# Weight sums made one block ahead, and on VectorE for one triple only; the first head pair's cache and queries split earlier; x at the head of the loads

## The chip, the cores and the metric

The kernel runs on one core of a Trainium2 chip. The metric is device time in microseconds (us) of one execution, of which lower is better. A core has a tensor engine (PE in the profile; PEld is its weight load), VectorE (DVE), ScalarE (ACT), GpSimd (POOL) and SyncE (SP), each with an instruction queue of its own that runs in order, and 16 DMA engines that are fed from the queues of SP and, in a few places, of ACT.

## The reference

One step of a streaming encoder with one layer (D = 1024), for a prompt of 1024 frames and a sample of 32 more, all of it float32. What the kernel must compute, cut to what matters here:

```python
mod = silu(c) @ w_ada + b_ada                 # c_prompt for the prompt, c_sample for the sample
sh1, sc1, gt1, sh2, sc2, gt2 = split(mod, 6)
h = rmsnorm(x, g_mix) * (1 + sc1) + sh1
u = h @ w_in        # attention q, k, v; mLSTM q, k, v, o and gates; two merge gates
ya = sample or prompt band attention(q, k, v, rel_bias)   # 8 heads of 64, 64-frame chunks, 8 past ones
ym = mLSTM(...)                                # 4 heads of 128
x = x + gt1 * ((sigmoid(ga) * (ya @ w_br_att) + sigmoid(gm) * (ym @ w_br_mlstm)) @ w_out)
h2 = rmsnorm(x, g_ffn) * (1 + sc2) + sh2
g, up = split(h2 @ w_gate_up, 2)               # D_FF = 2816, that is 22 blocks of 128
x = x + gt2 * ((silu(g) * up) @ w_down)
y = rmsnorm(x, g_final)
```

The new keys and values, the mLSTM states and the convolution rows are outputs as well.

## The kernel before

**Tokens and tiles.** Prompt and sample are worked on together as T = 1056 tokens, with channels on the partitions and tokens along the free axis, in three thirds of 352 tokens (`TILES`).

**Products.** Every large product is done in three passes. Each operand is split in two: the high part is a copy rounded to the `fp32r` type, the low part is the float32 value less that copy. The passes are high by high, low by high, high by low (`PASSES`). `split_to` (lines 392 to 395) makes the two parts of a weight block: ACT writes the high part at line 394, and at line 395 VectorE (or GpSimd) subtracts it from the raw block. The profile's rows for L394 and L395 are these two steps, for all weights.

**Order of the work.** PE, ACT, VectorE and GpSimd run their instructions in the order in which the program traces them. The order on SP is chosen by the framework. `Weights.advance` loads a weight block's DRAM rows ahead and traces its split so that at most four blocks are split and not used up; `W.use` calls it ahead of each product. So block n + 3 is split in trace order just ahead of the product of block n, and the copies of product n out of PSUM come behind that split. `Side` mixes jobs written as generators (attention, mLSTM, the rest of the modulation) into the products, a step at a time; short tasks in `side.later` are taken out one by one between the matmuls of a unit (lines 434 and 435: at k = 2, 4 and 6, so three to a unit).

**The start** (lines 215 to 353). SP issues `c_prompt` and `c_sample` (lines 216 and 217, rows of `prow`), then the first four of eight tiles of x (line 231), the other six parameter vectors (`param_loads`, lines 220 to 225, also rows of `prow`), x tiles 4 to 7, the sample's x (line 235), and w_ada (line 286). PE transposes x with the identity, for each group of four x tiles eight times four transposes (line 300); ACT copies each four out of PSUM (line 301); VectorE makes the sums of squares (line 295). Behind the first two fours of the second group, `param_cols` transposes `prow` (line 245), and ACT takes silu of c (line 247). Then `first_ada` multiplies w_ada, PE for the larger part of it (line 337) and VectorE for the rest (lines 341 and 343, summed by PE at line 351), with the splits of the first two input weights in the midst of it (L394, L395). `first_units` (line 460) is the first product with h.

**The first head pair** (`b_qkv(0)`, then `attention(0)`). `k_block`, `v_block` and `q_block` project keys, values and queries of two heads. `q_block(0)` calls `cache_loads` (line 572; the loads are at lines 609 to 611) and, behind its three units, puts `cache_kv` into `side.later` (line 586). `cache_kv` transposes the cached keys (line 620) and splits cached keys and values (lines 624 and 626, and `split_heads`, lines 545 and 546). The first step of `attention(0)` computes the low part of the scaled queries on VectorE, as two instructions over all 1056 tokens (lines 644 and 645, tile `q_low`). The scores (line 667) multiply the high and then the low queries with the keys; their row minimum is taken at line 681 on VectorE.

**The fifteen products** (class `Fifteen`, lines 1306 to 1368, and `fifteen_products`). For 18 of the 22 blocks of the feed-forward layer, three 128-column rows of w_gate_up are multiplied at a time with a form that needs fifteen block products instead of eighteen. There are twelve such triples. Each has fifteen weight blocks of 512 x 128; the first four are blocks as they are loaded, the other eleven are sums or differences of blocks, made in place in the raw tiles at line 1362 by the engine `self.eng`, directly ahead of the block's split:

```python
            def split(_):
                if 3 in loads:
                    self.load(3)
                if op is not None:
                    self.eng.tensor_tensor(a(dst), a(x), a(y), op=op)
                t = wsplit_tile()
                split_to(t, a(dst))
                return [t]
```

Line 1397 gives the first two triples VectorE and the other ten GpSimd. The split's low part (L395) is on VectorE in this part of the kernel. Each product is twelve matmuls (line 1725); its result is copied out by ACT (line 1761) or added or subtracted on VectorE (line 1763, once a copy at line 1759); finished thirds go through silu (line 1788) and are multiplied (line 1792). From the last plain unit to the ninth product of the first triple, `late_forms` splits the last twenty pieces of the other operand too (ACT at line 1574, VectorE at line 1577); all of them are traced ahead of the ninth product. Behind the triples come the last block, the down projection and the final norm, which the change leaves alone.

Of the kernel before, what the change touches and what calls it, by code (L numbers as in the profile page):

```python
# [12 lines left out]
ALU = mybir.AluOpType  # L13
# [4 lines left out]
P = 128  # L18
# [121 lines left out]
def hybrid_stream_step(  # L140
# [55 lines left out]
    def f(ap):  # L196
        return ap.bitcast(F32)
# [15 lines left out]


    prow = tmpt((P, P))
    sp.dma_start(prow[R_C:R_C + 8], c_prompt.rearrange("o (r c) -> (o r) c", c=P))
    sp.dma_start(prow[R_C + 8:R_C + 16], c_sample.rearrange("o (r c) -> (o r) c", c=P))
    xtok = []
    def param_loads():
        sp.dma_start(prow[R_ADA:R_ADA + 48], b_ada.rearrange("o (r c) -> (o r) c", c=P))  # L220
        sp.dma_start(prow[R_GMIX:R_GMIX + 8], g_mix.rearrange("o (r c) -> (o r) c", c=P))
        sp.dma_start(prow[R_GFFN:R_GFFN + 8], g_ffn.rearrange("o (r c) -> (o r) c", c=P))
        sp.dma_start(prow[R_GAIN:R_GAIN + 4], mh_gain.rearrange("o (r c) -> (o r) c", c=P))
        sp.dma_start(prow[R_CW:R_CW + 32], conv_w.rearrange("o j (r c) -> (o j r) c", c=P))
        sp.dma_start(prow[R_CB:R_CB + 8], conv_b.rearrange("o (r c) -> (o r) c", c=P))

    for i in range(KD):
        if i % 2 == 0:
# [298 lines left out]
    def v_block(hp):  # L527
        w = w_cols(VA + hp * P)

        def run():  # L530
            vf = tmpt()
            for lo, hi, pt in units(w):
                act.activation(vf[:, lo:hi], pt, AF.Copy)
            W.advance()
            side.later += [lambda: v_tail(hp, vf, 0), lambda: v_tail(hp, vf, 1), lambda: v_sample(hp, vf)]
        run.w = w
        return run

# [21 lines left out]
    def v_sample(hp, vf):  # L560
        vst = vst_t[hp] = ap_.tile([TS, 2, 2, DH], F32R, tag="vst", name=nm("vst"))
        stg = sample_tail(vf[:, S:T], new_v_s, hp)
        split_heads(vst, stg.rearrange("p (h d) -> p h d", h=2), dve)

    def q_block(hp):
        w = w_cols(QA + hp * P, None if hp else slots)

        def run():
            qt = att_q[hp] = slot([P, 2, T], F32R)
            raw = q_raw[hp] = tmpt()  # L570
            if hp == 0:
                ckv = cache_loads()
                ql = slot([P, 2, T], F32R)
                for hh, (u, v) in enumerate(ROWS):
                    pool.memset(f(ql[v, hh]), 0.0)
                q_low.append(ql)
            for lo, hi in TILES:
                pt = unit(w, 0, hs, lo, hi)
                act.activation(raw[:, lo:hi], pt, AF.Copy, scale=DH ** -0.5)

                for hh, (u, v) in enumerate(ROWS):
                    act.activation(qt[u, hh, lo:hi], pt[u], AF.Copy, scale=DH ** -0.5)
                for hh, (u, v) in enumerate(ROWS):
                    pool.tensor_scalar(qt[v, hh, lo:hi], f(qt[u, hh, lo:hi]), 1.0, 1.0, op0=ALU.mult, op1=ALU.mult)
            if hp == 0:
                side.later.append(lambda: cache_kv(ckv))
        run.w = w
        return run

# [48 lines left out]
    def attention(hp):  # L638
# [1 line left out]

        ck, cv = ckv_t
        kt, qt, vt, vst = att_k[hp], att_q[hp], att_v[hp], vst_t[hp]
        ql, raw = q_low[0], q_raw[hp]
        for hh, (u, v) in enumerate(ROWS):
            dve.tensor_tensor(ql[u, hh], raw[u], f(qt[u, hh]), op=ALU.subtract)
        yield
        yaT = tmpt()
        bts = {}
# [659 lines left out]
    class Fifteen:  # L1308
# [6 lines left out]
        def __init__(self, rows, eng):  # L1315
            self.rows, self.raw, self.eng = rows, {}, eng
            plus, minus = ALU.add, ALU.subtract
            p, q, r, s, t, u = [(i, j) for i in range(3) for j in range(2)]
            x = (3, 0)
            self.blocks = [  # L1320
                self.block(p, loads=(0, 1)),
                self.block(q),
                self.block(s, loads=(2,)),
                self.block(t),
                self.block(x, r, minus, s, loads=(3,)),
                self.block(r, p, minus, r),
                self.block(u, q, minus, u),
                self.block(r, r, plus, s),
                self.block(u, t, plus, u),
                self.block(s, s, minus, t),  # L1330
                self.block(t, q, minus, r),
                self.block(r, q, minus, u),
                self.block(p, p, minus, u),
                self.block(x, x, plus, s),
                self.block(s, s, minus, r),
            ]
# [12 lines left out]
        def block(self, dst, x=None, op=None, y=None, loads=()):  # L1349
# [5 lines left out]
                    if i < 3:  # L1355
                        self.load(i)

            def split(_):
                if 3 in loads:
                    self.load(3)  # L1360
                if op is not None:
                    self.eng.tensor_tensor(a(dst), a(x), a(y), op=op)  # L1362
                t = wsplit_tile()
                split_to(t, a(dst))
                return [t]
# [28 lines left out]
    w_f = [[weight([gate_up(c, fb)], KD, 3, slots if fb == 1 else None)  # L1394
            for c in range(2)] for fb in range(NPLAIN)]
    hk_rows = [gate_up(c, fb) for fb in range(NPLAIN, NF - 1) for c in range(2)]
    fifteen = [Fifteen(hk_rows[i:i + 3], dve if i < 6 else pool) for i in range(0, len(hk_rows), 3)]
    w_last = [last_blocks(gate_up(c, NF - 1)) for c in range(2)]

    def down(k0, k1, j):  # L1400
# [776 lines left out]
```

## Time and profile before

| | us |
|---|---|
| time, median of three runs (1637.7 to 1637.98) | 1637.95 |
| time of the profiled execution | 1636.14 |
| its span, first to last instruction | 1634.1 |
| PE busy | 1589.4 |
| VectorE busy | 1124.6 |
| ScalarE busy | 782.9 |
| GpSimd busy | 416.9 |

The mean granted clock of the tensor engine is 0.997. The profiled execution's time is 2.0 us above its span. A busy share of the tensor engine isn't a share of its peak: matmuls are pipelined, and one that stands alone shows 0.43 us where one in a row takes 0.16 us from start to start. Idle time of an engine counts only where PE waits for it in the end. In rows of the timeline the columns are start, duration, engine, line, operation, output <- input, shape, count, and in brackets the idle time ahead of it and what ended it. "L395" is line 395 of the kernel.

### The profile page before, as it was taken

What the parts mean: (1) busy time and instruction counts of PE and PEld (TensorE: products, weight loads), DVE (VectorE), ACT (ScalarE), POOL (GpSimd) and SP (SyncE); (2) the same over time, 40 slices, a digit from 0 to 9 for tenths busy, and PEclk for the clock granted to TensorE, in tenths of its full rate; (3) what the DMA queues carried; (4) which work ended last, traced back from release to release, by engine and by line L of the source; (5) the groups of instructions that cost most, each with busy time, mean ns of one, the idle gap of its engine ahead of it and who ended that gap; (6) DMA issues with size and microseconds to landing.
All of it is one profiled execution on the core that took longest, in us unless ns stands there. A gap on an engine that the chain in (4) does not pass through costs nothing.

```text
span 1634.1 us, 27464 instructions
## 1 busy us (share of the span) xinstructions
PE 1589.4 (97%) x10324; PEld 1564.6 (96%) x10324; DVE 1124.6 (69%) x2186; ACT 782.9 (48%) x1735; POOL 416.9 (26%) x451
## 2 busy tenths in 40 slices
PE   7989999999999999999999998899999999999997
PEld 6989999999999999999999997899999999999997
DVE  6756564546776744546655697789888886799754
ACT  3456454543455544443434555454454544545443
POOL 1234333334332311000012100056566560000001
PEclk9999999999999999999999999999999999999999
DMA  9732323232223332584453210222313227427454
GB/s 343 260 93 76 111 75 106 67 123 80 84 83 79 64 97 68 123 276 156 132 152 109 92 53 27 79 92 79 105 53 104 79 66 253 142 78 241 129 157 126
DMA packets 210326, 192.44 MB, mean 118 GB/s; under 512 B 10571, under 2 KB 180531, under 8 KB 209171
## 3 DMA queue, kind: packets, MB, share of 16 engines
q1 hardware_dynamic: 205554, 187.88, 36.9%
q10 hardware_dynamic: 4640, 2.82, 0.6%
q8 instruction: 81, 1.33, 0.3%
q14 instruction: 51, 0.41, 0.1%
HBM read 152.19 MB, written 41.63 MB: 119 GB/s over the span
## 4 chain that ended last, share of the span: by engine, by line
PE 85%; DVE 5%; ACT 3%; issue 1%; DMA 0%; ACTq 0%; POOL 0%; DVEq 0%; POOLq 0%
PE mm L428 39%; PE psb L1725 17%; PE mm L1725 9%; PE mm L2128 3%; PE mm L826 2%; PE psb L2128 2%; PE psV L725 2%; PE psb L1971 2%; PE psS L667 1%; PE psT L694 1%; PE mm L1971 1%; ACT wsp L394 1%; DVE wsp L395 1%; DVE st L681 1%; PE psV L1060 1%
## 5 line engine op out<-in xcount | busy, mean ns | idle before, releaser
L428 PE MATMUL mm<-s,wsp 128*128 128x352 f32 x4104 | 689.9, 324 | 2.1 <-DVE stg L518 1.6
L428 PEld LDWEIGHTS mm<-s,wsp 128*128 128x128 f32 x4104 | 656.9, 188 | 4.7 <-DVE stg L518 2.2
L395 DVE TENSOR_TENSOR wsp<-wraw,wsp 128x512 fp32r<-128x512 f32 (+1 forms) x284 | 234.1, 842 | 133.3 <-ACT wsp L394 131.6
L1725 PE MATMUL psb<-s,wsp 128*128 128x352 f32 x1611 | 273.5, 323 | 6.5 <-DVE t L1763 2.8
L394 ACT ACTIVATE wsp<-wraw 128x512 fp32r<-128x512 f32 x340 | 201.4, 617 | 156.0 <-PE psb L1725 40.4
L1725 PEld LDWEIGHTS psb<-s,wsp 128*128 128x128 f32 x1611 | 260.4, 188 | 9.5 <-ACT wsp L394 6.6
L1725 PE MATMUL mm<-s,wsp 128*128 128x352 f32 x933 | 161.3, 323 | 4.5 <-DVE wsp L395 1.7
L1725 PEld LDWEIGHTS mm<-s,wsp 128*128 128x128 f32 x933 | 151.1, 188 | 7.5 <-DVE wsp L395 3.2
L687 POOL TENSOR_SCALAR st<-st,mx 128x640 f32<-128x640 f32 (+5 forms) x72 | 56.2, 781 | 190.8 <-DVE mx L686 172.4
L1142 DVE SCALAR_TENSOR_TENSOR t<-wa,cmix,t 128x512 f32<-128x512 f32 x112 | 89.8, 807 | 11.9 <-DMA wa<-in_w_ada_dram 11.5
L395 POOL TENSOR_TENSOR wsp<-wraw,wsp 128x512 fp32r<-128x512 f32 x56 | 75.5, 1369 | 51.2 <-ACT wsp L394 50.7
L682 ACT ACTIVATE st<-st,mx 128x640 f32<-128x640 f32 (+5 forms) x72 | 47.9, 665 | 72.0 <-DVE mx L681 71.9
L681 DVE CUSTOM_DVE_ANT_0 st<-psS,bias 128x640 f32<-128x640 f32 (+5 forms) x72 | 44.5, 617 | 55.0 <-PE psS L667 42.6
L701 ACT ACTIVATE pT<-psT 128x640 fp32r<-128x640 f32 (+3 forms) x80 | 38.7, 494 | 69.2 <-PE psT L694 49.4
L1675 POOL TENSOR_TENSOR t<-t,sl 128x352 f32<-128x352 f32 x18 | 17.4, 968 | 185.3 <-ACT sl L1673 185.3
L2040 POOL TENSOR_TENSOR fst<-fst 128x1 f32<-128x1 f32 (+1 forms) x6 | 1.2, 192 | 236.9 <-ACT t L2033 236.9
L1362 POOL TENSOR_TENSOR spare<-wraw 128x512 f32<-128x512 f32 x10 | 14.5, 1447 | 172.4 <-DVE t L1763 138.7
L706 DVE TENSOR_TENSOR pT<-psT,pT 128x640 fp32r<-128x640 f32 (+3 forms) x80 | 44.0, 559 | 20.5 <-ACT pT L701 20.3
L826 PE MATMUL mm<-s,s 128*128 128x264 f32 (+3 forms) x432 | 54.8, 283 | 0.0
L2128 PE MATMUL mm<-s,wsp 128*128 128x352 f32 x330 | 54.4, 324 | 0.0
L2128 PEld LDWEIGHTS mm<-s,wsp 128*128 128x128 f32 x330 | 53.0, 188 | 0.0
L826 PEld LDWEIGHTS mm<-s,s 128*128 128x128 f32 (+1 forms) x432 | 51.9, 179 | 0.5
(384 smaller groups left out, 2539.2 us busy)
## 6 DMA issues: line engine op xcount, KB each, us to landing
wraw<-in_w_in_dram SPq DMA_DIRECT2D x40, 512.0 KB
wraw<-in_w_gate_up_dram SPq DMA_DIRECT2D x33, 512.0 KB
wa<-in_w_ada_dram SPq DMA_DIRECT2D x64, 256.0 KB
wraw<-in_w_down_dram SPq DMA_DIRECT2D x32, 512.0 KB
a_d<-t SPq DMA_DIRECT2D x22, 528.0 KB
g_d<-t SPq DMA_DIRECT2D x16, 528.0 KB
x<-xres SPq DMA_DIRECT2D x16, 528.0 KB
t<-g_d SPq DMA_DIRECT2D x16, 528.0 KB
```

The lines of the kernel that those rows point to most:

```text
L394: act.activation(dst[:, 0], src, AF.Copy)
L395: eng.tensor_tensor(dst[:, 1], src, f(dst[:, 0]), op=ALU.subtract)
L428: pe.matmul(pt[:, :hi - lo], wt[(w0 + k) // 4][:, a, (w0 + k) % 4], xt[k][:, b, lo:hi], start=(k == 0 and q == 0), stop=(k == n - 1 and q ...
L681: dve.tensor_tensor_reduce(so, sv, bi, -1.0, 3.0e38, ALU.add, ALU.min, mx[:n, 1:2])
L682: act.activation(st[:n, :w], st[:n, :w], AF.Exp, bias=mx[:n, 1:2], scale=-1.0, accum_out=mx[:n, 2:3])
L687: pool.tensor_scalar(st[:n, :w], st[:n, :w], mx[:n, 3:4], 1.0, op0=ALU.mult, op1=ALU.mult)
L706: dve.tensor_tensor(pv[:m, 1, a:b], pT[:m, a:b], f(pv[:m, 0, a:b]), op=ALU.subtract)
L826: pe.matmul(pt[:n, :wd], hs[k][:, a, i * P:i * P + n], whl[b][:, k, :wd], start=(k == 0 and q == 0), stop=(k == KD - 1 and q == 2))
L1142: dve.scalar_tensor_tensor(ac[:, c], wa, cmix[:, c, k:k + 1], ac[:, c], op0=ALU.mult, op1=ALU.add)
L1725: pe.matmul(acc, wt[:, a, k], x[k][:, b], start=(start and not onto and k == 0 and q == 0), stop=(stop and k == 3 and q == 2), skip_group_ ...
L1971: pe.matmul(acc, wt[k // 4][:, u, k % 4], piece_of[k, i][:, v], start=(k == 0 and q == 0), stop=(k == KP - 1 and q == 2))
L2128: pe.matmul(acc, wt[(k - k0) // 4][:, u, (k - k0) % 4], piece_of[k, 2][:, v], start=(k == 0 and q == 0), stop=(k == NF - 1 and q == 2))
```

## The change

1. **Sums.** Making a block's sum is taken out of `split` into `make`, and the makes are kept in a list. The split of block n first calls the make of block n + 1 of the same triple, then does its own two steps. So the sum of block n + 1 stands ahead of the low part of block n on VectorE, and one block earlier on GpSimd.
2. **Engine of the sums.** VectorE makes them in the first triple alone; the second triple's go to GpSimd, like those of the ten behind it.
3. **The first head pair.** `cache_loads` is called from `v_block(0)` and `cache_kv` is put into `side.later` behind that block's own three tasks, so that it is taken out in the third unit of `q_block(0)` instead of the first unit of `k_block(1)`. The low part of the queries of this pair is computed by thirds (`low_queries`, two instructions of 64 x 352 for each), each behind its unit in `q_block(0)`, and no longer in the first step of `attention(0)`. The other three pairs keep theirs.
4. **Loads.** The two c vectors go into `param_loads`, and all eight parameter loads are issued from ACT's queue. SP issues nothing ahead of the x tiles.

The hunks stand in the order of the code: the parameter loads, `v_block`, `low_queries`, `q_block`, the first step of `attention`, `Fifteen.block`, and the line that makes the triples. (In `Fifteen.__init__`, `self.sums = []` is added ahead of the blocks.)

```diff
@@ -213,16 +213,13 @@
     prow = tmpt((P, P))
-    sp.dma_start(prow[R_C:R_C + 8], c_prompt.rearrange("o (r c) -> (o r) c", c=P))
-    sp.dma_start(prow[R_C + 8:R_C + 16], c_sample.rearrange("o (r c) -> (o r) c", c=P))
     xtok = []
+
     def param_loads():
-        sp.dma_start(prow[R_ADA:R_ADA + 48], b_ada.rearrange("o (r c) -> (o r) c", c=P))
...
-        sp.dma_start(prow[R_CB:R_CB + 8], conv_b.rearrange("o (r c) -> (o r) c", c=P))
+        for row, src in ((R_C, c_prompt), (R_C + 8, c_sample), (R_ADA, b_ada), (R_GMIX, g_mix), (R_GFFN, g_ffn),
+                         (R_GAIN, mh_gain), (R_CB, conv_b)):
+            act.dma_start(prow[row:row + src.shape[-1] // P], src.rearrange("o (r c) -> (o r) c", c=P))
+        act.dma_start(prow[R_CW:R_CW + 32], conv_w.rearrange("o j (r c) -> (o j r) c", c=P))
...
@@ -529,10 +526,14 @@
         def run():
             vf = tmpt()
+            if hp == 0:
+                ckv = cache_loads()
             for lo, hi, pt in units(w):
                 act.activation(vf[:, lo:hi], pt, AF.Copy)
             W.advance()
             side.later += [lambda: v_tail(hp, vf, 0), lambda: v_tail(hp, vf, 1), lambda: v_sample(hp, vf)]
+            if hp == 0:
+                side.later.append(lambda: cache_kv(ckv))
...
@@ -562,6 +563,10 @@
+    def low_queries(hp, lo, hi):
+        for hh, (u, v) in enumerate(ROWS):
+            dve.tensor_tensor(q_low[0][u, hh, lo:hi], q_raw[hp][u, lo:hi], f(att_q[hp][u, hh, lo:hi]), op=ALU.subtract)
...
@@ -569,7 +574,6 @@
             if hp == 0:
-                ckv = cache_loads()
...
                 for hh, (u, v) in enumerate(ROWS):
                     pool.tensor_scalar(qt[v, hh, lo:hi], f(qt[u, hh, lo:hi]), 1.0, 1.0, op0=ALU.mult, op1=ALU.mult)
-            if hp == 0:
-                side.later.append(lambda: cache_kv(ckv))
+                if hp == 0:
+                    low_queries(hp, lo, hi)
...
@@ -640,9 +644,9 @@
-        ql, raw = q_low[0], q_raw[hp]
-        for hh, (u, v) in enumerate(ROWS):
-            dve.tensor_tensor(ql[u, hh], raw[u], f(qt[u, hh]), op=ALU.subtract)
+        ql = q_low[0]
+        if hp:
+            low_queries(hp, 0, T)
         yield
...
@@ -1355,11 +1360,19 @@
-            def split(_):
+            def make():
                 if 3 in loads:
                     self.load(3)
                 if op is not None:
                     self.eng.tensor_tensor(a(dst), a(x), a(y), op=op)
+
+            n = len(self.sums)
+            self.sums.append(make)
+
+            def split(_):
+
+                for f in self.sums[n + 1:n + 2]:
+                    f()
                 t = wsplit_tile()
                 split_to(t, a(dst))
                 return [t]
...
-    fifteen = [Fifteen(hk_rows[i:i + 3], dve if i < 6 else pool) for i in range(0, len(hk_rows), 3)]
+    fifteen = [Fifteen(hk_rows[i:i + 3], dve if i < 3 else pool) for i in range(0, len(hk_rows), 3)]
```

More of the change, by code (lines that the diff above doesn't have):

```diff
@@ L215, in hybrid_stream_step @@
     prow = tmpt((P, P))
-    sp.dma_start(prow[R_C:R_C + 8], c_prompt.rearrange("o (r c) -> (o r) c", c=P))
-    sp.dma_start(prow[R_C + 8:R_C + 16], c_sample.rearrange("o (r c) -> (o r) c", c=P))
     xtok = []
     def param_loads():
-        sp.dma_start(prow[R_ADA:R_ADA + 48], b_ada.rearrange("o (r c) -> (o r) c", c=P))
[L221 to L225, printed above, removed]
+        for row, src in ((R_C, c_prompt), (R_C + 8, c_sample), (R_ADA, b_ada), (R_GMIX, g_mix), (R_GFFN, g_ffn),
+                         (R_GAIN, mh_gain), (R_CB, conv_b)):
+            act.dma_start(prow[row:row + src.shape[-1] // P], src.rearrange("o (r c) -> (o r) c", c=P))
+        act.dma_start(prow[R_CW:R_CW + 32], conv_w.rearrange("o j (r c) -> (o j r) c", c=P))
     for i in range(KD):
@@ L1319, in __init__ @@
             x = (3, 0)
+            self.sums = []
             self.blocks = [
```

## Prediction, made before the change ran

> **What bounds the kernel now.** I read the page first (parts 1 and 2), then the waits of PE, then busy time by stretches, and then the timeline of the three places where PE has gaps. Page, part 1:
>
> ```profile
> PE 1589.4 (97%) x10324; PEld 1564.6 (96%) x10324; DVE 1124.6 (69%) x2186; ACT 782.9 (48%) x1735; POOL 416.9 (26%) x451
> ```
>
> PE is busy for 1589.4 of 1634.1 us, so an edit gains only where it takes a gap out of PE. Busy time by stretches (start:end, length, then busy us of PE, PEld, DVE, ACT, POOL, granted clock, DMA share, GB/s) shows where they are:
>
> ```profile
> 90.00:100.00 10.00, 7.80 (x48) 7.33 (x48) 7.80 (x16) 4.19 (x9) 2.23 (x6) 1.00 0.23 59
> 800.00:900.00 100.00, 100.00 (x631) 100.00 (x630) 55.79 (x100) 41.47 (x84) 16.22 (x16) 1.00 0.41 128
> 1000.00:1050.00 50.00, 41.27 (x231) 36.74 (x230) 37.03 (x69) 21.34 (x45) 0.00 (x0) 1.00 0.14 43
> 1050.00:1100.00 50.00, 46.91 (x284) 45.43 (x284) 42.91 (x65) 22.91 (x46) 22.20 (x14) 1.00 0.30 97
> 1600.00:1635.00 35.00, 24.51 (x162) 23.90 (x160) 14.25 (x26) 12.22 (x35) 4.60 (x14) 0.90 0.35 111
> ```
>
> PE is full from 800 to 900, for one, and has gaps at 90 to 100 (2.2 us), in 1000 to 1100 (8.7 and 3.1) and at the end (10.5 to 1635, which the change doesn't touch). The longest entry among PE's waits is the load of x (total, times, longest):
>
> ```profile
> PE mm L300 <- DMA s<-in_x_prompt_dram: 10.3, 6, 5.2
> ```
>
> The change goes at the start, at 90 to 100 and at 1000 to 1064. Busy time understates the last: the stretches of the first three triples there hold the same number of matmuls.
>
> ```profile
> 988.40:1029.60 41.20, 32.91 (x182) 28.81 (x181) 30.99 (x59) 18.98 (x41) 0.00 (x0) 1.00 0.21 64
> 1029.60:1064.00 34.40, 30.72 (x181) 28.78 (x180) 25.39 (x45) 13.57 (x27) 2.01 (x2) 1.00 0.21 63
> 1064.00:1093.10 29.10, 29.10 (x182) 28.82 (x181) 26.54 (x40) 14.41 (x29) 17.33 (x12) 1.00 0.28 92
> ```
>
> The third triple, with its sums on GpSimd, takes 29.10 us with PE full. The first takes 12.1 us more, the second 5.3. That 17.4 us is the largest thing the change can reach.
>
> **Part 1: sums a block ahead, first triple.** One round of the timeline:
>
> ```profile
> 1008.21 0.68 DVE L1362 TENSOR_TENSOR wraw<-wraw,wraw 128x512 f32<-128x512 f32 x1
> 1008.99 0.63 ACT L394 ACTIVATE wsp<-wraw 128x512 fp32r<-128x512 f32 x1 [1.47 <-DVE wraw L1362]
> 1009.65 0.69 DVE L395 TENSOR_TENSOR wsp<-wraw,wsp 128x512 fp32r<-128x512 f32 x1 [0.76 <-ACT wsp L394]
> ```
>
> VectorE makes a sum, ScalarE waits for it and copies the high part, and VectorE stands still for 0.76 us until it may subtract. The groups of VectorE within 988.4 to 1029.6 (count, busy, mean ns, then idle time ahead of them and its releaser) total it:
>
> ```profile
> L395 DVE TENSOR_TENSOR wsp<-wraw,wsp 128x512 fp32r<-128x512 f32 x13 | 8.9, 690 | 6.8 <-ACT wsp L394 6.8
> L1577 DVE TENSOR_TENSOR x<-x,x 128x352 fp32r<-128x352 f32 x9 | 4.5, 521 | 1.2 <-ACT x L1574 1.2
> L395 DVE TENSOR_TENSOR wsp<-spare,wsp 128x512 fp32r<-128x512 f32 x2 | 1.4, 692 | 1.5 <-ACT wsp L394 1.5
> ```
>
> Of VectorE's 10.2 idle us (41.20 less 30.99), 8.3 are this wait. After the change the next sum (0.68) stands between, while ScalarE copies (0.63) from a sum that is a round old, so the 8.3 go. Then VectorE needs 41.2 - 8.3 = 32.9 for this stretch, and PE 29.1. VectorE is last only while the late pieces (L1577) lie among its work. In the chain of work, which counts VectorE's instructions from start to start, a copy out of PSUM is 0.43 and a sum 0.61:
>
> ```profile
> 1004.08 0.86 DVE row L1763 x2
> 1005.81 0.61 DVE wraw L1362
> ```
>
> After the ninth product a block costs VectorE a sum, a low part of the same shape and about one copy, 0.61 + 0.61 + 0.43, near 1.7, against twelve matmuls in 29.1 / 15 = 1.94 on PE; over six blocks that returns up to 1.4. I take 32.0: **9.2 gained**. Most: 12.1, PE's floor. Least: 4, half of the waits, if ScalarE's copy then waits behind its own evictions instead. Nothing is below zero here: no instruction is added, and neighbouring blocks never write the same tile, so the sum moved ahead finds its inputs ready (the tile that it overwrites was split two blocks earlier or more).
>
> **Part 2: second triple's sums on GpSimd.** Busy time of VectorE in the first two stretches by the sums (L1362), and in the second and third by the low parts (L395):
>
> ```profile
> 988.40:1029.60 41.20, 7.54 (x11) 1.00 0.21 64
> 1029.60:1064.00 34.40, 7.53 (x11) 1.00 0.21 63
> ```
>
> ```profile
> 1029.60:1064.00 34.40, 10.76 (x14) 1.00 0.21 63
> 1064.00:1093.10 29.10, 16.70 (x17) 1.00 0.28 92
> ```
>
> VectorE loses 7.53 us of sums; GpSimd takes 17.33 / 12 = 1.44 for one, 15.9 for eleven, which PE's 29 us hide. VectorE's own low parts get longer beside it: 0.98 mean in the third triple against 0.77. So the second triple should look like the third: 34.4 becomes 29.2, **5.2 gained** (most 5.3). What comes late next is the row load that the sums wait for; the third triple lives with it and has no gap in PE.
>
> [...]
>
> **Part 3: the first pair.** PE's two gaps there, with what surrounds them:
>
> ```profile
> 78.42 0.42 SPq L610 DMA_DIRECT2D t<-in_cache_v_dram  x1
> 88.10 0.60 PE L620 MATMUL mm<-ident,t 128*128 128x128 f32 x4
> 90.58 1.39 DVE L626 TENSOR_TENSOR s<-mm,s 64x512 fp32r<-64x512 f32 x2 [5.41 <-ACT s L624]
> 93.07 2.53 DVE L645 TENSOR_TENSOR s<-t,s 64x1056 fp32r<-64x1056 f32 x2
> 94.37 0.33 PE L667 MATMUL psS<-s,s 128*128 128x128 f32 x1 [1.27 <-DVE s L645]
> 96.15 1.06 DVE L502 TENSOR_TENSOR s<-mm,s 64x352 fp32r<-64x352 f32 x2
> 97.24 0.29 DVE L681 CUSTOM_DVE_ANT_0 st<-psS,bias 128x128 f32<-128x128 f32 x1
> 97.59 0.50 PE L667 MATMUL psS<-s,s 128*128 128x256 f32 x2 [0.93 <-DVE mx L681]
> ```
>
> The first gap, 1.27, is the low queries; the second, 0.93, is the row minimum at 97.24, which is late because L645 pushed L502 back. VectorE was idle for 5.41 us just before. The moved work is the two cache loads, the cache's transposes, copies and subtractions, and six subtractions of 64 x 352 in place of two (L502's pair of that shape is 1.06, so 3.2 for 2.53, 0.7 more). All of it fits in the 5.41 and in ScalarE's pauses. The transposes move from 88.1 to about 84, still 5 us behind the issue of the last cache load at 78.4. Behind the new subtractions on VectorE are queued the next unit's value splits and then L502; PE waits for those only if VectorE is full, and it isn't. I take 2.0 of 2.2: **2.0 gained**; most 2.2, least -0.7 (the added work all on the path).
>
> **Part 4: x first.**
>
> ```profile
> 0.79 0.40 SPq L216 DMA_DIRECT2D t<-in_c_prompt_dram  x1
> 1.56 1.78 SPq L231 DMA_DIRECT2D s<-in_x_prompt_dram  x4
> 5.16 0.45 PE L300 MATMUL mm<-ident,s 128*128 128x128 f32 x1 [5.16 <-DMA s<-in_x_prompt_dram]
> 6.79 0.27 SPq L225 DMA_DIRECT2D t<-in_conv_b_dram  x1
> 8.07 2.64 SPq L231 DMA_DIRECT2D s<-in_x_prompt_dram  x4
> 9.45 5.61 PE L300 MATMUL mm<-ident,s 128*128 128x128 f32 x31 [0.87 <-DMA s<-in_x_prompt_dram]
> 9.96 0.60 ACT L301 ACTIVATE s<-mm 128x512 f32<-128x512 f32 x1 [7.89 <-PE mm L300]
> 17.60 0.77 PE L300 MATMUL mm<-ident,s 128*128 128x128 f32 x5 [1.43 <-DMA s<-in_x_prompt_dram]
> 32.26 1.15 ACT L394 ACTIVATE wsp<-wraw 128x512 fp32r<-128x512 f32 x2 [3.82 <-DMA wraw<-in_w_in_dram]
> 76.69 0.44 ACTq L525 DMA_DIRECT2D out_dram<-stg  x1
> ```
>
> SP's twelfth issue (L225, 6.79) starts just as a tile of x lands, and the fifth x only at 8.07; so SP stood still behind eight loads in flight, six of them small. Without the small ones all eight x tiles go out from 0.79: 0.77 earlier, the first four at their old spacing (9.45 - 5.16) / 3 = 1.43, the fourth (which PE had at 9.45) at 8.7, and the rest at that spacing too, the last at 14.4 instead of 17.60. PE's first 31 transposes take 5.61, so from 8.7 they end at 14.3, beside the last landing. That is 3.2; some transposes were done in the waits before, so I take **3.1 gained**. It holds to the end of the start only if the w_ada and w_in stream, which ScalarE awaits at 32.26, moves too; it follows x in the same queue, so it should. Most 3.9 (if the transposes also hurry), least 0. ScalarE now issues eight loads of up to 0.44, 3.5 us; behind them is queued its first copy, which comes at 9.96 and isn't due before 9. Should its last issues wait for x tiles to land, as SP's did, that costs ScalarE some 0.4 there.
>
> **Sum.** 9.2 + 5.2 + 2.0 + 3.1 = 19.5. The profiled execution took 1636.14 (span 1634.1 and 2.0 around it), so 1616.6; it lies 1.8 below the median of the three runs, 1637.95, from which I forecast 1618.5. Its own range is 1615 to 1623: all parts but the first at their most and that one at 11 (22.4), or 6, 4.8, 1.5 and 2.3 (14.6). A measurement of this kernel can tell a change of 0.2%, 3.3 us, from none.
>
> **Rivals.**
> - *ScalarE takes VectorE's place in the first triple* (its copies queue behind evictions that wait for PE). Part 1 gives 4: 1623.7. For: it is in the round with two engines already. Against: 18.98 busy of 41.20.
> - *The start is hidden*: w_in's landing at 32.26 doesn't move and the splits behind it set the start's end. Part 4 gives nothing: 1621.6. For: ScalarE's 3.82 of waiting. Against: one queue, served in order.
> [...]
> - *The sums aren't ahead after all*: each waits for the round of the block before, and VectorE's 8.3 only change place. Part 1 gives nothing: 1627.7. Against: the tiles' order in part 1.
> - *Slower:* with its gaps closed, PE is granted less clock from 988 to the end, 646 us. Each hundredth costs 6.5 us; it turns the gain into a loss of 3.3 from a mean of 0.965 down: 1641.2 there. For: the last stretch's 0.90. Against: 800 to 900, PE full at 1.00.
>
> **How the numbers follow.** Forecast 0.58; ScalarE 0.17; start hidden 0.12; second triple bound 0.07; sums not ahead 0.04; slower 0.02. The range reaches down to all parts at their most (12.1 + 5.3 + 2.2 + 3.9 = 23.5, 1614.5), and up over the first three rivals to 1626; it leaves out some 0.15: the last two rivals, and two of the first three at once. Faster by over 0.2%: all but the last, with 0.01 for no change: 0.97, 0.01, 0.02.
>
> **What would show it.** First triple 31 to 33 us, VectorE's wait for L394 under 2; second triple 29 to 29.5 with GpSimd at 15 or more; no wait of PE for L645, and the first two scores with no gap; the last x transposes near 14.4, the first matmul of `first_units` near 45 instead of 48. I am wrong if the first triple stays over 36, or if the time is above 1626.

## The result, and the profile after

The changed kernel takes 1624.96 us (median; 1624.17 to 1626.35) against 1637.97 beside it: a ratio of 0.9919, interval 0.9902 to 0.9936. That is faster by 13.0 us, where 19.5 were forecast. The profiled execution took 1624.59, with a span of 1622.9.

Part 1 of the page, and then stretches in the columns of before:

```profile
PE 1586.7 (98%) x10324; PEld 1567.1 (97%) x10324; DVE 1123.9 (69%) x2179; ACT 782.9 (48%) x1735; POOL 434.7 (27%) x462
```

```profile
90.00:100.00 10.00, 6.13 (x39) 5.85 (x38) 3.55 (x6) 2.91 (x5) 3.85 (x5) 1.00 0.51 168
1000.00:1050.00 50.00, 48.09 (x296) 47.06 (x295) 47.43 (x79) 27.41 (x56) 18.86 (x12) 1.00 0.22 67
1050.00:1100.00 50.00, 50.00 (x313) 50.00 (x313) 43.77 (x61) 25.62 (x52) 31.14 (x21) 1.00 0.22 73
```

From 1000 on PE is nearly full now (296 matmuls in 50 us, 231 before). From 90 to 100 it is emptier than before: 39 matmuls against 48. The first three triples:

```profile
992.60:1024.30 31.70, 29.79 (x182) 28.76 (x181) 30.00 (x59) 18.82 (x41) 1.82 (x1) 1.00 0.28 83
1024.30:1053.20 28.90, 28.90 (x182) 28.90 (x182) 27.20 (x37) 13.73 (x27) 20.15 (x13) 1.00 0.24 75
1053.20:1082.10 28.90, 28.90 (x182) 28.90 (x182) 25.82 (x38) 14.74 (x29) 16.99 (x12) 1.00 0.28 93
```

The same 182 matmuls take 31.7 and 28.9 us (41.2 and 34.4 before). VectorE's groups in the first of these stretches (count, busy, mean ns, then idle ahead and its releaser; the low part of the split is L392 now, the late pieces L1590):

```profile
L392 DVE TENSOR_TENSOR wsp<-wraw,wsp 128x512 fp32r<-128x512 f32 x13 | 9.6, 736 | 0.0
L1590 DVE TENSOR_TENSOR x<-x,x 128x352 fp32r<-128x352 f32 x9 | 4.5, 522 | 1.1 <-ACT x L1587 1.1
```

The 6.8 us of waiting for ScalarE's copy are gone. The two longest entries among PE's waits (total, times, longest):

```profile
PE mm L297 <- DMA s<-in_x_prompt_dram: 10.6, 5, 4.5
PE psS L671 <- DVE mx L685: 5.1, 2, 4.7
```

The wait for x is what it was (10.3 before), and there is a new one, of 4.7 us, for a row minimum of the first head pair.

**Where the time went.** Four marks of PE cut each profiled execution into stretches: the first matmul of `first_units`, the last score matmul of `attention`, the first matmul of the fifteen products and the last of the down projection. The table holds every run told of below too; the ratio is to the kernel before beside it. One of the five executions of x_stream took 3905.7 us, a slow one; its median counts it.

| run | time, us | ratio, interval | start to first_units | to last score | to first triple | to last down |
|---|---|---|---|---|---|---|
| before | 1637.97 | 1 | 48.0 | 401.0 | 539.4 | 635.2 |
| after | 1624.96 | 0.9919, 0.9902 to 0.9936 | 48.1 | 403.5 | 541.0 | 619.9 |
| after_again | 1625.06 | 0.9919, 0.9906 to 0.9931 | 48.1 | 404.0 | 541.0 | 619.9 |
| sums_only | 1621.82 | 0.9899, 0.9886 to 0.9913 | 48.8 | 401.6 | 539.3 | 619.9 |
| t1_only | 1623.05 | 0.9909, 0.9896 to 0.9923 | 49.6 | 401.8 | 539.4 | 619.9 |
| t2_only | 1633.31 | 0.9968, 0.9958 to 0.9979 | 48.5 | 401.3 | 539.4 | 629.6 |
| q_only | 1618.47 | 0.9880, 0.9867 to 0.9894 | 48.5 | 398.6 | 539.4 | 620.0 |
| cache_only | 1625.45 | 0.9924, 0.9911 to 0.9938 | 48.3 | 406.3 | 539.4 | 619.9 |
| no_x | 1625.74 | 0.9924, 0.9911 to 0.9938 | 48.8 | 404.2 | 541.0 | 619.9 |
| pair_rb_v | 1621.12 | 0.9901, 0.9886 to 0.9917 | 48.5 | 399.0 | 540.9 | 620.0 |
| x_first_sp | 1624.27 | 0.9914, 0.9900 to 0.9927 | 49.9 | 401.2 | 540.9 | 619.9 |
| x_stream | 1630.72 | 0.9954, 0.9941 to 0.9968 | 56.5 | 400.9 | 539.3 | 620.0 |
| q_pool | 1616.99 | 0.9870, 0.9857 to 0.9884 | 46.2 | 399.2 | 539.5 | 619.9 |
| q_pool_ada8 | 1618.68 | 0.9877, 0.9861 to 0.9894 | 49.5 | 398.4 | 539.4 | 619.9 |

From before to after the four stretches give +0.1, +2.5, +1.6 and -15.3, together -11.1; the spans differ by 11.2. (The medians differ by 13.0; before's profiled execution lay 1.8 below its median.) The eight kernels that load the start as before begin `first_units` between 48.0 and 49.6, so a single value of that column is good to some 0.8. The second repeats within 0.9 where nothing in it was changed, the last two within 0.2, but for the step of 1.6 in the third, which the run after_again explains.

The theory from here: the triples gave all of the gain; the first pair cost 2.5 by a changed order on SP's queue; x at the head gave nothing because ScalarE's loads took its places in flight. The rivals: that the triples gave less and the pair cost nothing in the end; that VectorE's added work, not the queue, costs in the pair; that the landing of x is bound by the DMA engines.

### The profile page after: what moved, and what is told of

It is laid out like the page before. It is cut to its first block, busy times and chain, and to the rows that moved or that the text cites. A ratio compares the mean times of both kernels' runs of the same rounds, so it can differ in the third digit from the quotient of the medians.

```text
span 1622.9 us, 27478 instructions
## 1 busy us (share of the span) xinstructions
PE 1586.7 (98%) x10324; PEld 1567.1 (97%) x10324; DVE 1123.9 (69%) x2179; ACT 782.9 (48%) x1735; POOL 434.7 (27%) x462
## 4 chain that ended last, share of the span: by engine, by line
PE 90%; DVE 4%; ACT 2%; DMA 1%; issue 1%; POOL 0%; ACTq 0%; SPq 0%; DVEq 0%; POOLq 0%
PE mm L425 40%; PE psb L1738 18%; PE mm L1738 10%; PE mm L2141 3%; PE mm L830 3%; PE psb L2141 2%; PE psV L729 2%; PE psb L1984 2%; PE psS L671 1%; PE psT L698 1%; PE mm L1984 1%; PE psT L334 1%; PE mm L457 1%; DMA s<-in_x_prompt_dram 1%; DVE st L685 1%
## 5 line engine op out<-in xcount | busy, mean ns | idle before, releaser
L392 DVE TENSOR_TENSOR wsp<-wraw,wsp 128x512 fp32r<-128x512 f32 (+1 forms) x284 | 237.4, 853 | 125.8 <-ACT wsp L391 123.7
L392 POOL TENSOR_TENSOR wsp<-wraw,wsp 128x512 fp32r<-128x512 f32 x56 | 75.9, 1375 | 51.8 <-ACT wsp L391 51.4
L1367 POOL TENSOR_TENSOR wraw<-wraw,raw 128x512 f32<-128x512 f32 x33 | 55.7, 1702 | 0.9
```

The costliest lines, as they stand in the source:

```text
L392: eng.tensor_tensor(dst[:, 1], src, f(dst[:, 0]), op=ALU.subtract)
```

## The experiments

**Sums alone (sums_only).** Parts 3 and 4 undone, the diff of `Fifteen` kept:

```diff
+            self.sums.append(make)
...
+                for f in self.sums[n + 1:n + 2]:
+                    f()
...
-    fifteen = [Fifteen(hk_rows[i:i + 3], dve if i < 6 else pool) for i in range(0, len(hk_rows), 3)]
+    fifteen = [Fifteen(hk_rows[i:i + 3], dve if i < 3 else pool) for i in range(0, len(hk_rows), 3)]
```

> The kernel before with parts 1 and 2 alone (sums one block ahead, second triple's sums on GpSimd); loads and first pair as before. Theory (the triples gave all of the gain and the first pair took back some 2 to 3 us): first triple 31 to 32 us and second 29, so 15.1 us less than before, 1622.9, which is about 2 us faster than the changed kernel. Rival (the triples gave only the 13.0 that shows at the end of the kernel, and the first pair's new wait is made up later): 1625, the same as the changed kernel.

1621.82, that is 15.7 below before and 3.1 below the changed kernel. The last stretch has the whole 15.3. So the changed kernel with its parts 3 and 4 is 3 us slower; 1.6 of that is the step in the third stretch, and the second has 1.9.

**The two halves of part 3 (q_only, cache_only).** Each is sums_only with one half:

```diff
+                if hp == 0:
+                    low_queries(hp, lo, hi)
...
-        low_queries(hp, 0, T)
+        if hp:
+            low_queries(hp, 0, T)
```

> Parts 1 and 2, and of part 3 only the low queries by thirds; the cache's loads and its splitting stand where they stood before. In the queue of SP the first w_ada and bias loads of attention then stand ahead of the weight load again. Theory (the loss is that queue's order, brought by the early cache loads): no wait of over 1 us for the row minimum, the old gaps of 1.27 and 0.93 gone or smaller, 1 to 2 us faster than the kernel with the sums alone. Rival (the loss is the added VectorE work, six subtractions in place of two, which push the row minimum): the loss of 2 to 3 us against the sums alone stays here.

```diff
             vf = tmpt()
+            if hp == 0:
+                ckv = cache_loads()
...
+            if hp == 0:
+                side.later.append(lambda: cache_kv(ckv))
...
```

> Parts 1 and 2, and of part 3 only the cache's earlier loads and earlier splitting; the low queries stay in the first step of attention. In the queue of SP the first w_ada and bias loads stand behind a weight load that waits for GpSimd, as in the changed kernel. Theory (queue order): those two loads issue near 94 instead of 80, PE waits 4 us or more for a row minimum near 100, and the kernel is 2 to 3 us slower than the one with the sums alone. Rival (VectorE's added subtractions of the queries): no such wait, and the same as the sums alone or up to 1 us faster.

The low queries by thirds gain 3.35 us (1618.47), the early cache loses 3.6 (1625.45). The theory holds; the rival, VectorE's added work, falls. In q_only VectorE does the six subtractions (L567) in pauses, and PE has neither of the old gaps:

```profile
79.14 1.07 DVE L567 TENSOR_TENSOR s<-t,s 64x352 fp32r<-64x352 f32 x2 [1.04 <-ACT s L586]
86.29 1.04 DVE L567 TENSOR_TENSOR s<-t,s 64x352 fp32r<-64x352 f32 x2
88.60 1.24 DVE L567 TENSOR_TENSOR s<-t,s 64x352 fp32r<-64x352 f32 x2 [1.27 <-ACT s L586]
91.48 1.39 DVE L632 TENSOR_TENSOR s<-mm,s 64x512 fp32r<-64x512 f32 x2 [1.65 <-ACT s L630]
```

In cache_only this wait of PE is longer than in any other of these kernels, and the clock is low behind it (the second fence: a stretch in the columns of above):

```profile
102.45 0.79 PE L671 MATMUL psS<-s,s 128*128 128x256 f32 x2 [5.63 <-DVE mx L685]
```

```profile
102.00:107.00 5.00, 4.54 (x16) 4.55 (x17) 2.56 (x11) 2.34 (x7) 0.92 (x2) 0.50 0.19 57
```

**The order on SP's queue (no_x, pair_rb_v).** The chain in the changed kernel, from its timeline: GpSimd's low part of a weight block, SP's weight load that waits for it, behind that the first w_ada row and bias of attention, VectorE's first use of the w_ada row, then the row minimum, then PE.

```profile
90.67 2.98 POOL L392 TENSOR_TENSOR wsp<-wraw,wsp 128x512 fp32r<-128x512 f32 x2
```

```profile
93.67 0.40 SPq L401 DMA_DIRECT2D wraw<-in_w_in_dram  x1
94.12 0.57 SPq L1141 DMA_DIRECT2D wa<-in_w_ada_dram  x1
94.75 0.42 SPq L637 DMA_DIRECT2D bias<-rb_d  x1
```

```profile
98.87 0.49 DVE L1144 TENSOR_SCALAR t<-wa,cmix 128x512 f32<-128x512 f32 x1 [6.38 <-DMA wa<-in_w_ada_dram]
99.39 1.06 DVE L499 TENSOR_TENSOR s<-mm,s 64x352 fp32r<-64x352 f32 x2
100.47 0.29 DVE L685 CUSTOM_DVE_ANT_0 st<-psS,bias 128x128 f32<-128x128 f32 x1
```

```profile
93.83 0.34 PE L671 MATMUL psS<-s,s 128*128 128x128 f32 x2
100.83 0.79 PE L671 MATMUL psS<-s,s 128*128 128x256 f32 x2 [4.70 <-DVE mx L685]
```

In the kernel before, those two loads went out at 80.1 and 80.6, ahead of the weight load. The order on SP is the framework's, and the early cache loads changed it. No_x is the changed kernel with part 4 undone:

```diff
+    sp.dma_start(prow[R_C:R_C + 8], c_prompt.rearrange("o (r c) -> (o r) c", c=P))
...
-            act.dma_start(prow[row:row + src.shape[-1] // P], src.rearrange("o (r c) -> (o r) c", c=P))
...
```

> The changed kernel with part 4 undone: parts 1, 2 and 3 as they are in it, the parameter loads and x in the order of before. Theory (part 4 gives nothing, because loads in flight are counted over both queues; the first pair costs 3 us net): 1625, the same as the changed kernel within 1 us, and about 3 us over the 1621.8 of the sums alone. Rival (x at the head does help, or hurts, by something that the first matmul of first_units doesn't show): 2 us or more away from the changed kernel.

1625.74, as the changed kernel within 1 us. Pair_rb_v is no_x with one load traced earlier:

```diff
             if hp == 0:
+                rb_load()
                 ckv = cache_loads()
...
         sp.dma_start(ckv[:, 1], cache_v[0, 0].rearrange("t h d -> t (h d)"))
-        sp.dma_start(rb_d, bass.AP(rel_row.tensor, rel_row.offset, [[FLEN, H], [0, P], [1, FLEN]]))
```

> The kernel of the run no_x (parts 1, 2 and the whole of part 3) with one line moved: the load of the relative bias row is traced just ahead of the two cache loads and not behind them. No instruction of a computing engine changes; on the queue of SP the first w_ada and bias loads of attention then stand ahead of the weight load that waits for GpSimd. Theory (that order is the whole of the loss): those loads issue near 80 again, no wait of over 1 us for the first row minima, and 1618.5, 3 us less than the sums alone and over 6 less than the run no_x. Rival (the early splitting of the cache on VectorE, ScalarE and PE itself costs): the wait for the row minimum stays or moves, 1622 or more.

1621.12, so the order alone was worth 4.6. In SP's queue the two loads stand at 80 again and the weight load behind them, and VectorE runs from its low queries (L572) straight to the first use of w_ada:

```profile
79.74 0.41 SPq L1147 DMA_DIRECT2D wa<-in_w_ada_dram  x1
80.21 0.42 SPq L643 DMA_DIRECT2D bias<-rb_d  x1
...
93.95 0.39 SPq L404 DMA_DIRECT2D wraw<-in_w_in_dram  x1
```

```profile
91.16 3.15 DVE L572 TENSOR_TENSOR s<-t,s 64x352 fp32r<-64x352 f32 x2
94.34 0.49 DVE L1150 TENSOR_SCALAR t<-wa,cmix 128x512 f32<-128x512 f32 x1
```

The time missed its 1618.5: 2.65 more than q_only. The table puts 1.5 of that into the third stretch, in which the two kernels are the same; in the second, 399.0 stands beside 398.6. So with the order mended the early cache costs nothing that shows in its place, and it gains nothing over the low queries alone.

**x first (x_first_sp).** Sums_only, with all eight parameter loads behind all of x on SP:

```diff
-        if i == 3:
-            param_loads()
     xsm = tmpt((TS, D))
     sp.dma_start(xsm, xs_in)
+    param_loads()
...
```

> Parts 1 and 2, and x truly first: all eight x tiles and the sample's x on the queue of SP ahead of all eight parameter loads, which follow on the same queue. Theory (at most eight loads are in flight over both queues, and in the changed kernel the parameter loads of ScalarE took the places): all eight x tiles are issued from 0.8 to about 6 us with no wait between, the last transposes start near 14.4 instead of 17.5, the first product with h near 45, and the time is about 3 us less than with the sums alone, 1619.8. Rival (the landing of x is bound by the DMA engines or the memory, whatever the issue): the tiles are issued early, but the last transposes still start near 17 and the time is that of the sums alone. Second rival (the stream of w_ada and w_in sets the end of the start): last transposes near 14.4, first product with h near 48 still.

1624.27, slower than sums_only by 2.4, which no theory had: 1.6 of it is the step in the third stretch, and 1.1 lies in the start (`first_units` at 49.9). For the changed kernel, PE's timeline, and then SP's waits up to 20 us (total, times, longest):

```profile
8.09 0.47 PE L297 MATMUL mm<-ident,s 128*128 128x128 f32 x1 [1.80 <-DMA s<-in_x_prompt_dram]
11.34 5.55 PE L297 MATMUL mm<-ident,s 128*128 128x128 f32 x32 [2.78 <-DMA s<-in_x_prompt_dram]
17.55 0.77 PE L297 MATMUL mm<-ident,s 128*128 128x128 f32 x5 [0.66 <-DMA s<-in_x_prompt_dram]
```

```profile
SPq L228 <- DMA s<-in_x_prompt_dram: 2.7, 1, 2.7
SPq L228 <- DMA t<-in_b_ada_dram: 1.2, 1, 1.2
```

For x_first_sp, the timelines of SP and of PE:

```profile
0.79 3.87 SPq L228 DMA_DIRECT2D s<-in_x_prompt_dram  x8
4.71 0.45 SPq L230 DMA_DIRECT2D t<-in_x_sample_dram  x1
5.79 0.33 SPq L221 DMA_DIRECT2D t<-in_c_prompt_dram  x1
...
14.77 2.58 SPq L282 DMA_DIRECT2D s<-in_w_ada_dram  x5
```

```profile
8.37 6.84 PE L296 MATMUL mm<-ident,s 128*128 128x128 f32 x37 [0.81 <-DMA s<-in_x_prompt_dram]
...
37.33 3.63 PE L333 MATMUL psT<-csil,s 128*128 128x128 f32 x16 [3.16 <-DMA s<-in_w_ada_dram]
```

Eight x tiles leave SP without a wait, the ninth load waits for the first tile to land, the tenth for the second. In the changed kernel SP waits with x for `b_ada`, a load of ScalarE (it lands at 5.96, and the fourth x tile goes out at 5.97): the eight places hold for both queues. The places are completion semaphores: in the trace each load of SP or ScalarE names one of eight, the same eight for both, and waits until the load that named it before has landed. So that half of the theory stands, and PE transposes x without a wait from 8.37 on. But the eight small loads now go out one by one as x tiles land, most of them 1.28 us apart, w_ada starts at 14.77 (11.23 before), and PE loses at w_ada what it won at x. A part of the loss is the clock: behind the wait of 3.16 us sixteen matmuls take 3.63 us, where the sixteen of the next products take 1.95, and the granted clock is 0.51 from 38 to 41. What the DMA engines moved from 0 to 50 us, 1.25 us a figure, for before and x_first_sp:

```profile
GB/s 0 7 193 406 387 416 312 125 334 305 318 383 344 308 400 419 419 419 433 413 426 426 389 324 299 304 369 426 419 419 426 418 319 307 285 298 369 413 412 416
```

```profile
GB/s 0 52 324 410 416 423 419 419 416 413 201 5 85 262 406 419 426 419 419 413 419 433 426 327 290 316 330 409 439 419 419 426 320 299 297 295 371 410 406 419
```

In the first the last x tile has landed by 17.6, in the second by 13.9; from 17 us on the two rows are alike. A new theory: the start ends when 13.8 MB (x, w_ada and two blocks of w_in) are through, so only a hole in this row can be won, and x first opened one at 12.5 to 16. For the kernel before, it doesn't hold as it stands: there PE goes through the eight products with w_ada from 23.43 to 44.0 without waiting for a row, and the late x sets when they start. Only with x early is w_ada what PE waits for.

**Filling the hole (x_stream).** x_first_sp with two w_ada rows ahead of the parameters:

```diff
-    param_loads()
...
+    load_ada(2)
+    param_loads()
     load_ada(5)
```

> Parts 1 and 2, and SP's order x (eight tiles), sample's x, two rows of w_ada, the eight parameter loads, the rest of w_ada. Theory (the start is bound by the bytes that the DMA engines move, 14 MB from x to the last row of w_ada at some 420 GB/s; x first on its own only left them idle from 12.5 to 16 behind small loads): no such hole, last w_ada row 2 to 3 us earlier than in the run x_first_sp, the first matmul of first_units near 47, 1 to 1.8 us faster than the sums alone. Rival (the parameters come later now, and with them silu of c and the start of the products with w_ada): first_units at 49 or later, slower than the sums alone.

1630.72, the rival: the parameters land late, and PE, in order, stands in front of their transpose.

```profile
21.39 0.44 PE L240 MATMUL psV<-ident,t 124*128 124x124 f32 x1 [6.59 <-DMA t<-in_conv_w_dram]
```

**The parameters on GpSimd's queue (q_pool).** q_only with all of x at the head of SP, and the parameter loads, from the changed kernel's form:

```diff
-            act.dma_start(prow[row:row + src.shape[-1] // P], src.rearrange("o (r c) -> (o r) c", c=P))
+            pool.dma_start(prow[row:row + src.shape[-1] // P], src.rearrange("o (r c) -> (o r) c", c=P))
```

> Parts 1 and 2, the low queries by thirds (the run q_only), and x truly first with the eight parameter loads on the queue of GpSimd, which neither stands between x and w_ada on SP nor, by the order of the waits, shares its loads in flight. Theory (the start is bound by the bytes that the DMA engines move, and a small load costs only by the place it holds): x and w_ada at 400 GB/s or more from 2.5 on without a hole, last x transposes near 14.4, silu of c early, the first matmul of first_units near 46.5 instead of 48.5, and 1616.5, 2 us less than the run q_only. Rival (the products with w_ada are bound by PE and VectorE, or wait for something else): first_units at 48 or later, 1618.5. Second rival (GpSimd issues too slowly, so that the parameters come late): PE waits for the transpose of the parameters as in the run x_stream, 1620 or more.

1616.99, the fastest of all: 8.0 us below the changed kernel and 1.5 below q_only (the start shows 2.3). GpSimd issues its eight from 1.88 to 6.33; SP sends x without a wait and w_ada from 5.86; the row has a short dip to 275 where the hole was; the parameters' transpose comes at 15.37 and `first_units` at 46.2.

```profile
0.81 3.83 SPq L228 DMA_DIRECT2D s<-in_x_prompt_dram  x8
...
5.86 5.87 SPq L281 DMA_DIRECT2D s<-in_w_ada_dram  x5
```

```profile
GB/s 0 92 318 403 400 411 403 411 386 413 374 275 419 419 433 426 419 426 419 433 394 307 288 341 357 417 426 426 426 391 320 294 294 301 372 425 416 412 416 419
```

```profile
15.37 0.27 PE L240 MATMUL psV<-ident,t 124*128 124x124 f32 x1
```

**All of w_ada ahead of w_in (q_pool_ada8).**

```diff
-    load_ada(5)
+    load_ada(KD)
...
-            if k == 3:
+            if k == 6:
                 W.advance()
```

> The run q_pool with two lines changed: all eight rows of w_ada are loaded ahead of the first two weight blocks of w_in, and the splits of those two stand behind the seventh of the eight products with w_ada, not behind the fourth. Theory (in q_pool the last three products with w_ada still wait 1.3 us in all for their rows, which stand behind 1 MB of w_in): the eight products run without a wait, first_units near 45 instead of 46.2, and 1615.8. Rival (the splits now come so late that VectorE and ScalarE finish them behind the sums of the products): first_units at 46.5 or later, 1617 to 1619.

1618.68, no gain, and `first_units` at 49.5: the rival. PE's eight products run without a wait and end at 40.8, but VectorE's splits stand ahead of its last product with w_ada, and the sums wait for that. The clock adds to it: it is 0.50 from 43 to 53.

```profile
38.26 1.30 DVE L391 TENSOR_TENSOR wsp<-wraw,wsp 128x512 fp32r<-128x512 f32 x2 [3.00 <-ACT wsp L390]
39.97 1.29 DVE L391 TENSOR_TENSOR wsp<-wraw,wsp 128x512 fp32r<-128x512 f32 x2 [0.41 <-ACT wsp L390]
41.18 1.94 DVE L339 SCALAR_TENSOR_TENSOR t<-s,csil,t 128x768 f32<-128x768 f32 x2
```

**Parts 1 and 2 apart (t1_only, t2_only).** t1_only is sums_only with `dve if i < 6 else pool`; t2_only is the kernel before with `dve if i < 3 else pool`.

> Part 1 alone: sums one block ahead in all triples, but VectorE still makes those of the second triple too; loads and first pair as before. Theory (part 2 is worth its 5.2 us by itself): first triple 31 to 32, second still near 34, so some 5 us slower than parts 1 and 2 together, 1627. Rival (the order alone closes the second triple as well, as its block costs VectorE 1.7 us against 1.94 on PE once the wait for ScalarE is gone): second triple under 31, and 1622 to 1623, within 1 us of parts 1 and 2 together.

> Part 2 alone: the second triple's sums go to GpSimd, and all sums stand in the split as before; loads and first pair as before. Theory (part 2 is a gain by itself, and was only not needed beside part 1): first triple 41, second 29, 5.3 us less than before, 1632.4. Rival (without the order, GpSimd's sum stands in the round and ScalarE and PE wait for it): second triple still over 33, 1636 or more.

t1_only has the whole 15.3 without part 2 (1623.05; of its 1.2 over sums_only, 0.8 lies in the start, within its scatter). t2_only has 5.6 of it. The second triple of each:

```profile
1023.00:1052.00 29.00, 29.00 (x182) 29.00 (x182) 27.38 (x48) 13.78 (x28) 4.45 (x3) 1.00 0.24 74
```

```profile
1030.40:1059.60 29.20, 29.20 (x182) 28.99 (x181) 27.50 (x40) 15.01 (x29) 17.38 (x12) 1.00 0.25 75
```

Either change alone closes the second triple; the two overlap, and beside part 1, part 2 is worth nothing that can be measured.

**The changed kernel again (after_again).**

> The changed kernel once more, unaltered. Its first profile shows a granted clock of 0.83 from 920 to 930 us, in a stretch where PE is full and nothing was changed; three other kernels show it there too, and the kernel before and four others don't. Theory (the dip belongs to the kernel, and costs it 1.6 us each time): it is there again, and the time is 1625. Rival (it falls on single executions by chance): no dip, or one elsewhere, and single times that scatter by 1.6 us with it.

1625.06, and the dip from 920 to 930 is there again: 66 matmuls in 10 us, beside 71 in sums_only (after_again first).

```profile
920.00:930.00 10.00, 10.00 (x66) 10.00 (x65) 4.20 (x13) 4.66 (x8) 1.65 (x1) 0.83 0.64 195
```

```profile
920.00:930.00 10.00, 10.00 (x71) 10.00 (x71) 5.15 (x16) 5.04 (x10) 1.65 (x1) 1.00 0.53 157
```

Four kernels have the 1.6 in the third stretch (the changed one, no_x, pair_rb_v, x_first_sp), the others don't, and the theory that it belongs to the kernel doesn't follow from that. What sets it off can be read from the traces. The second norm makes 24 matmuls with a single output column each, here from 919.70 to 922.08 in the changed kernel; behind them the clock is at half (the second fence):

```profile
919.70 0.28 PE L1526 MATMUL psV<-ones,t 128*128 128x1 f32 x2
...
922.08 3.19 PE L425 MATMUL mm<-s,wsp 128*128 128x352 f32 x12
```

```profile
923.00:926.00 3.00, 3.00 (x12) 3.00 (x12) 1.04 (x8) 0.65 (x1) 1.65 (x1) 0.50 0.97 279
```

All fourteen profiled executions have this stretch of 24 matmuls, 2.38 us long. In the traces the clock changes only on a grid of windows of 3.41 us (in the changed kernel it is 0.50 from 49.10 to 52.52, from 100.31 to 103.72 and from 922.92 to 926.33, in the kernel before from 47.65 to 51.06; the changed kernel's three starts are 15 and 241 windows apart), which lies differently against the start of each execution. In the five executions with the dip, 2.00 us or more of the stretch fall into one window (all 2.38 in four of them), and the half rate starts where that window ends; in the nine without it at most 1.95 do. So the 1.6 is set by where the stretch falls on the clock's grid, not by one of the four parts. Both traced executions of the changed kernel fall alike, with the window beginning 0.2 and 0.4 us ahead of the stretch; whether that is more than chance, two can't tell.

## Why the prediction was right and wrong, point by point

- **Part 1** (first triple 41.2 to 32.0): right, 31.7, with no wait for the high part left in VectorE's largest group. What it missed is that the same step closes the second triple. The sum had the number for it: a block costs VectorE 1.7 us against 1.94 on PE, and it was used for the first triple alone.
- **Part 2** (34.4 to 29.2): right in place and size, 28.9 with GpSimd at 20.15, but counted as if it added to part 1. That GpSimd's sums lengthen VectorE's low parts is seen and hidden: the low part in the second triple takes 1.16 us (mean of ten) in sums_only and 0.86 in t1_only, and PE is full in both. In the changed kernel each of the 88 low parts of 128 x 512 that start while GpSimd makes a sum ends 0.55 us after that sum does (0.69 is its length alone), so a low part meets only the rest of a sum, or none. No run with its sums on GpSimd shows the second triple bound by VectorE, to which the prediction gives 0.07: it took 28.9 here and 29.2 in t2_only, with PE full in both.
- **Part 3** (2.0 gained): the step that failed. The low queries did what was said and a bit more (2.4 to 3.0 by the second column, 3.35 by the time). The cache was costed on PE, ScalarE and VectorE, and its two loads at nothing. They and the load of the bias row were moved, the framework then put the first loads of attention behind a weight load that waits for GpSimd, and that order cost 4.6. "Least -0.7" looked only at VectorE.
- **Part 4** (3.1 gained): failed at "without the small ones all eight x tiles go out from 0.79". The prediction saw eight loads in flight on SP and took the limit for that queue's own. ScalarE's loads hold the same places. Its second step failed as well: x_first_sp brings x early and gains nothing, as w_ada follows no earlier. The rival "start hidden" has the right time for this part (0.7 to 0.8 gained by no_x, within the start's scatter), for another reason than the landing of w_in that it named.
- **The clock.** The rival "slower" is not what happened, but the clock took part: 1.6 at 920, which no part of the change causes, and at most 1.7 behind the new gap.
- **Sum.** By stretches, forecast and measured: start -3.1 and +0.1, pair -2.0 and +2.5, between 0 and +1.6, triples -14.4 and -15.3. The forecast's own range, 1615 to 1623, was missed. The time of 1624.96 lies in the wider one because its upper end took in three rivals, and none of them is what happened: that the range held is luck, since parts 3 and 4 failed in their mechanism.

## What to carry to other kernels

A load that is moved is priced by the queue it is moved in: list what stands behind it there, and what the places in flight are shared with, before counting the work that it feeds. Where a stage is bound by the bytes that must arrive, look for holes in the DMA row; putting all of w_ada ahead of w_in, with no hole to fill, gained nothing here. Two edits that remove the same wait don't add up: price the second on the profile that the first would leave. Before a difference of a us or two gets a cause, cut the span into stretches and look at the clock in each: 1.6 of what parts 3 and 4 seemed to cost came from a stretch that they don't touch.

## What the runs showed of the hardware

- Two gaps in PE cost more than their length. Behind the 4.70 of the changed kernel the clock is 0.83 over the ten us from 100, 1.7 us of clock lost; behind the 5.63 of cache_only it is 0.66 over the same ten, 3.4 lost. In the trace of the changed kernel the 1.7 is one window of 3.41 at 0.50, from 100.31 to 103.72; the 3.4 is twice as much.
- PE can be busy in the profile and still lose its clock: behind 24 matmuls of one output column the clock fell to half when 2.00 us or more of them lay in one window of 3.41, and not when 1.95 or less did. Behind the 2.38 that lay whole in the window up to 922.92 of the changed kernel, it was 0.50 from there to 926.33. That these matmuls set it off is inferred from these fourteen executions; no run moved the stretch on purpose.
- In these programs a load of SP or ScalarE waits for the load that had its completion semaphore before, one of eight for both queues, whatever the size: a load of 4 KB holds a place as one of 512 KB does (in the trace of the changed kernel the fourth x tile, of 512 KB, takes the place of `b_ada`, 24 KB, and waits 1.2 us for it, and the fifth that of `g_mix`, 4 KB). GpSimd's loads take none of these places: in q_pool five of them and SP's eight x tiles, thirteen loads, have been issued ahead of 4.7, when the first x tile lands. As far as the traces show it, the limit is one of how the programs are built, and not of the chip. With the small loads on GpSimd the first row of w_ada went out at 5.86, beside 9.55 with them on ScalarE and 14.77 with them on SP. SP's eight issues of 0.25 to 0.33 each are only 2.3 of the 8.9 between 5.86 and 14.77; that the rest is places saved is the author's estimate from these figures.
